# The turning frame of a state-space unit, from two tables of factors

## The chip, the cores and the metric

The kernel runs on one core of one Trainium2 chip. The metric is the device time of one execution in microseconds; the time of a kernel is the median of its runs, and the profiled execution's own time and span stand beside it. The engines are TensorE (PE, with its weight loads as PEld), VectorE (DVE), ScalarE (ACT), GpSimd (POOL) and SyncE (SP), which issues the DMAs.

## The reference, cut to what matters

One layer of a decoder for 512 tokens of width 2048 in float32: RMS norm, one input projection, two mixers side by side, an output projection with residual, a gated convolutional MLP, and a last norm. The change lies in the second mixer, S5, a diagonal state space of 64 groups with 64 complex states each:

```python
def s5_mixer(u, a_re, a_im, log_dt, b_re, b_im, c_re, c_im, d, w_glu, b_glu):
    A = lax.complex(a_re, a_im)
    dt = jnp.exp(log_dt)[:, None]
    A_bar = jnp.exp(A * dt)
    B_bar = ((A_bar - 1.0) / A)[..., None] * Bm
    Bu = jnp.einsum('gpc,btgc->btgp', B_bar, uf)
    ...
    _, states = lax.associative_scan(combine, (a, Bu), axis=1)
    y = jnp.real(jnp.einsum('gcp,btgp->btgc', Cm, states)) + d * uf
```

The recurrence `s[t] = A_bar s[t-1] + Bu[t]` is complex. The kernel runs it in a turning frame: `A_bar` is a size R times a turn `e^(i theta)`. Multiplied by the inverse of its own turn so far, the state follows a real recurrence with R alone, which DVE's scan instruction does for the real and the imaginary part; the result is turned back afterwards. Four tokens are taken together, so a step of the frame is the turn of four tokens, and there are 128 of them.

## The kernel before

**Matmuls.** Every float32 product is taken apart into a high and a low part and done as three matmuls (`mm3`, L208 to L210). ACT casts the high part of a weight chunk (L115), DVE subtracts for the low part (L116), and PE reads both. PE's work comes in dense chunks: first the projection `u` in two halves of four tiles (`upt`, 5 PSUM banks under the tag acc), then the other projections `xm`, `v`, `o`, later the output projection and the MLP.

**S5 beside it.** S5 is a Python generator, `s5()`, which the dense code advances by `pump()` after a chunk. So the engines' instruction orders are fixed when the program is built, and S5's small steps lie between dense chunks on each engine's queue. It begins with `s5_params()` (L360 to L441): from the parameters DVE works out the turn of one token for all 32 pairs of groups, and POOL squares it twice and then doubles it six times. That is the **EM chain** (L323 and L329 of POOL): seven levels of the turn by 1, 2, 4, ... 64 steps, real and imaginary, 32 columns each. They are kept in `prms`, one buffer of 512 columns, together with two weights `W0`.

**A unit.** Eight units of four pairs each follow. `phases(u)` (L463 to L489) makes the frame of a unit: `Er` and `Ei`, 4 pairs x 128 steps = 512 columns each, by doubling: one memset each, a copy of one step (L476, L477), then six levels of six POOL operations each (L482 to L487) which take the first m steps times the turn by m steps and write the next m. `Rd`, the sizes, is made by ACT (L468) and one memset of POOL (L469). The unit then makes its input coefficients (L515 to L528), multiplies them on PE into PSUM tiles `px` (L612), turns `px` by the frame on DVE (L619 to L624, into `vr`, `vi`), computes taps on PE (`pkt`, L636), scans and turns back (L639 to L648). `phases(u+1)` is called in the middle of unit u, just ahead of the buffers `ta`, `tb`, `vr`, `vi`; so the frame of a unit is made one unit ahead.

**Tokens.** When a half of `u` is complete, `u_tokens` evicts its four PSUM tiles, scaled, into four buffers `utok` (L293 to L300): even tiles by DVE (L300), odd ones by ACT (L298), four instructions each. The first half is evicted behind chunk 15, while PE goes on with the second half.

**Buffers.** `slot()` takes the oldest free buffer of 128x512 from a queue and `drop()` puts one back at its end. There are 13 float32 ones inside two larger areas, used first, and 60 more. A buffer that comes back from the queue makes its first writer wait for its last readers, whatever engine they are on.

## Time and profile before

| | us |
|---|---|
| median of 3 runs | 2100.53 (2099.14 to 2102.38) |
| profiled execution | 2100.77 |
| its span | 2099.0 |
| PE busy | 2055.1 |
| DVE busy | 1502.0 |
| ACT busy | 819.4 |
| POOL busy | 275.6, in 512 instructions |

The granted clock of PE is 0.99 over the whole span. PE is busy for 98% of it; the other engines are not, and what they do matters where PE waits for them. POOL's work lies mostly before 350 us, in the EM chain and the eight `phases`. The chain of waits that ended last is 83% PE and 9% DVE.

### The profile page before, as it was taken

What the parts mean: (1) busy time and instruction counts of PE and PEld (TensorE: products, weight loads), DVE (VectorE), ACT (ScalarE), POOL (GpSimd) and SP (SyncE); (2) the same over time, 40 slices, a digit from 0 to 9 for tenths busy, and PEclk for the clock granted to TensorE, in tenths of its full rate; (3) what the DMA queues carried; (4) which work ended last, traced back from release to release, by engine and by line L of the source; (5) the groups of instructions that cost most, each with busy time, mean ns of one, the idle gap of its engine ahead of it and who ended that gap; (6) DMA issues with size and microseconds to landing.
All of it is one profiled execution on the core that took longest, in us unless ns stands there. A gap on an engine that the chain in (4) does not pass through costs nothing.

```text
span 2099.0 us, 31618 instructions
## 1 busy us (share of the span) xinstructions
PE 2055.1 (98%) x12956; PEld 1874.6 (89%) x12956; DVE 1502.0 (72%) x2101; ACT 819.4 (39%) x1033; POOL 275.6 (13%) x512
## 2 busy tenths in 40 slices
PE   8999988999999999999999999999999999999997
PEld 8898877888888899999999999999999888888887
DVE  8698986557755799898899899889886544222235
ACT  5244332445423544444443444344343432211225
POOL 4874732002100200000000000000000000000003
PEclk9999999999999999999999999999999999999998
DMA  4222121222333423333333333433332555332352
GB/s 175 82 86 74 63 84 51 91 89 83 126 121 121 150 105 126 128 111 121 111 115 125 123 111 111 134 118 111 121 111 102 190 178 188 115 112 107 113 200 81
DMA packets 75370, 244.74 MB, mean 117 GB/s; under 512 B 8396, under 2 KB 14028, under 8 KB 64216
## 3 DMA queue, kind: packets, MB, share of 16 engines
q1 hardware_dynamic: 75224, 242.72, 33.8%
q8 instruction: 101, 1.65, 0.3%
q14 instruction: 45, 0.37, 0.1%
HBM read 220.12 MB, written 22.57 MB: 116 GB/s over the span
## 4 chain that ended last, share of the span: by engine, by line
PE 83%; DVE 9%; issue 3%; ACT 2%; POOL 2%; DMA 1%; SPq 0%; DVEq 0%; ACTq 0%; POOLq 0%
PE gv L210 14%; PE gv L208 14%; PE gv L209 14%; PE down L209 6%; PE down L210 6%; PE down L208 6%; DVE a L116 2%; PE o L208 1%; PE ws L208 1%; PE o L210 1%; PE ws L210 1%; PE o L209 1%; PE ws L209 1%; PE u L208 1%; PE u L209 1%
## 5 line engine op out<-in xcount | busy, mean ns | idle before, releaser
L210 PE MATMUL gv<-T,a 128*128 128x256 f32 x2408 | 682.2, 283 | 4.9 <-DVE a L1176 4.9
L208 PE MATMUL gv<-T,a 128*128 128x256 f32 x2408 | 682.1, 283 | 0.0
L209 PE MATMUL gv<-T,a 128*128 128x256 f32 x2408 | 682.0, 283 | 0.0
L1172 ACT CAST a<-a 128x1536 fp32r<-128x1536 f32 (+2 forms) x171 | 291.0, 1703 | 458.1 <-PE gv L209 295.7
L210 PEld LDWEIGHTS gv<-T,a 128*128 128x128 f32 x2408 | 463.0, 192 | 5.1 <-DVE a L1176 5.1
L208 PEld LDWEIGHTS gv<-T,a 128*128 128x128 f32 x2408 | 462.9, 192 | 0.0
L209 PEld LDWEIGHTS gv<-T,a 128*128 128x128 f32 x2408 | 462.9, 192 | 0.0
L116 DVE TENSOR_TENSOR a<-a,a 128x1024 fp32r<-128x1024 f32 (+2 forms) x207 | 241.1, 1169 | 288.3 <-ACT a L115 287.6
L1176 DVE TENSOR_TENSOR a<-a,a 128x1536 fp32r<-128x1536 f32 (+2 forms) x173 | 348.0, 2012 | 37.9 <-ACT a L1172 37.9
L115 ACT CAST a<-a 128x1024 fp32r<-128x1024 f32 (+2 forms) x208 | 199.8, 967 | 361.4 <-PE down L209 284.5
L1525 POOL TENSOR_TENSOR c<-c,c 128x256 f32<-128x256 f32 x24 | 17.7, 739 | 1318.5 <-ACT c L1523 1318.2
L208 PE MATMUL down<-c,a 128*128 128x512 f32 x448 | 174.5, 390 | 0.6 <-ACT c L115 0.6
L210 PE MATMUL down<-c,a 128*128 128x512 f32 x448 | 174.3, 389 | 0.0
L209 PE MATMUL down<-c,a 128*128 128x512 f32 x416 | 162.1, 390 | 0.9 <-DVE c L116 0.9
L1158 DVE TENSOR_TENSOR a<-a 128x1024 f32<-128x1024 f32 x85 | 103.6, 1219 | 0.0
L208 PEld LDWEIGHTS down<-c,a 128*128 128x128 f32 x448 | 84.1, 188 | 18.7 <-ACT c L115 1.4
L210 PEld LDWEIGHTS down<-c,a 128*128 128x128 f32 x448 | 84.1, 188 | 17.3
L209 PEld LDWEIGHTS down<-c,a 128*128 128x128 f32 x416 | 78.1, 188 | 17.7 <-DVE c L116 1.5
L209 PE MATMUL down<-a,a 128*128 128x512 f32 x176 | 68.5, 389 | 0.0
L208 PE MATMUL down<-a,a 128*128 128x512 f32 x176 | 68.5, 389 | 0.0
L1237 DVE SCALAR_TENSOR_TENSOR p<-p,vec,p 128x511 f32<-128x511 f32 x86 | 62.6, 748 | 2.5 <-ACT p L1230 0.9
L1164 DVE TENSOR_TENSOR a<-a 128x512 f32<-128x512 f32 x86 | 60.5, 704 | 2.9
(578 smaller groups left out, 3590.0 us busy)
## 6 DMA issues: line engine op xcount, KB each, us to landing
a<-in_wgv SPq DMA_DIRECT2D x86, 1024.0 KB, 4.8
a<-in_wdB SPq DMA_DIRECT2D x55, 512.0 KB, 3.5
a<-in_wdA SPq DMA_DIRECT2D x40, 320.0 KB, 3.1
hidd<-p SPq DMA_DIRECT2D x40, 256.0 KB, 5.4
a<-in_wxm SPq DMA_DIRECT2D x16, 512.0 KB, 3.2
a<-in_wv SPq DMA_DIRECT2D x16, 512.0 KB, 3.3
a<-in_wo SPq DMA_DIRECT2D x16, 512.0 KB, 3.3
a<-in_wouts SPq DMA_DIRECT2D x16, 512.0 KB, 3.5
```

What stands on the lines that cost most here:

```text
L115: S.copy(out=h, in_=src)
L116: V.tensor_tensor(out=l, in0=src, in1=f(h), op=SUB)
L208: PE.matmul(pt, lhsT=wh, rhs=xh, start=first, stop=False)
L209: PE.matmul(pt, lhsT=wh, rhs=xl, start=False, stop=False)
L210: PE.matmul(pt, lhsT=wl, rhs=xh, start=False, stop=last)
L1158: eng.tensor_tensor(out=v[:, 4:6], in0=v[:, 3:4].to_broadcast([P, 2, T]), in1=v[:, 0:2], op=ADD)
L1164: V.tensor_tensor(out=v[:, 3], in0=v[:, 6], in1=v[:, 2], op=ADD)
L1172: S.copy(out=part(RH[s % 2], lo, hi - lo), in_=part(RS[s % 2], lo, hi - lo))
L1176: V.tensor_tensor(out=part(RL[s % 2], lo, hi - lo), in0=part(RS[s % 2], lo, hi - lo), in1=f(part(RH[s % 2], lo, hi - lo)), op=SUB)
L1237: V.scalar_tensor_tensor(out=y1[:, s:], in0=gs[:, 0:T - s], scalar=vcol("f_cw", 3 * (k0 + j) + 2 - s), in1=y1[:, s:], op0=MUL, op1=ADD)
L1525: G.tensor_tensor(out=x2, in0=x2, in1=sq[:, 0:HT], op=ADD)
```

## The change

**Tables.** A frame of 128 steps is the product of two short ones: step 16a + b is step 16a times step b, with a from 0 to 7 and b from 0 to 15. `factors()` makes both tables once for all 32 pairs, at the end of the EM chain: `FB` (b, 16 entries x 32 pairs, 512 columns in each of two buffers) and `FA` (a, 8 entries x 32 pairs, real and imaginary halves of one buffer). Both come from `turns()`, the doubling of before with 32 pairs in place of 4: 46 instructions of POOL, four of them memsets. It then drops its scratch `gt` and `prms`; `W0` moves into spare columns of `cst`. Three buffers are held to the end of S5.

**Units.** `phases(u)` is now six operations of 512 columns, each with one factor broadcast along a and one along b; the memset and ACT's operation for `Rd` stay.

**Place.** `phases(u+1)` is called at the end of unit u, behind the drop of its buffers.

```diff
--- before.py
+++ after.py
@@ -357,6 +357,35 @@
 
     W0, EM, R4 = [], [], []
 
+    def turns(er, ei, lev0, n, gt):
+
+        G.memset(er[:, :, 0:1], 1.0)
+        G.memset(ei[:, :, 0:1], 0.0)
+        m, lev = 1, lev0
+        while m < n:
+            br, bi = [EM[lev][q].unsqueeze(2).to_broadcast([P, NPAIR, m]) for q in range(2)]
+            h1, h2 = [gt[:, o:o + NPAIR * m].rearrange("p (r n) -> p r n", r=NPAIR) for o in (0, 256)]
+            lo, hi = slice(0, m), slice(m, 2 * m)
+            G.tensor_tensor(out=h1, in0=er[:, :, lo], in1=br, op=MUL)
+            G.tensor_tensor(out=h2, in0=ei[:, :, lo], in1=bi, op=MUL)
+            G.tensor_tensor(out=er[:, :, hi], in0=h1, in1=h2, op=SUB)
+            G.tensor_tensor(out=h1, in0=er[:, :, lo], in1=bi, op=MUL)
+            G.tensor_tensor(out=h2, in0=ei[:, :, lo], in1=br, op=MUL)
+            G.tensor_tensor(out=ei[:, :, hi], in0=h1, in1=h2, op=ADD)
+            m, lev = 2 * m, lev + 1
+
+    FB, FA, held = [], [], []
+
+    def factors():
+
+        fbr, fbi, fa, gt = [slot(name=n) for n in ("fbr", "fbi", "fa", "gt")]
+        held.extend([fbr, fbi, fa])
+        FB.extend(t.rearrange("p (r b) -> p r b", r=NPAIR) for t in (fbr, fbi))
+        FA.extend(t.rearrange("p (r a) -> p r a", r=NPAIR) for t in (fa[:, 0:256], fa[:, 256:512]))
+        turns(*FB, 0, 16, gt)
+        turns(*FA, 4, 8, gt)
+        drop(gt, prms)
+
     def s5_params():
 
         a_re, a_im, ldt = vcol("a_re", 0, 32), vcol("a_im", 0, 32), vcol("log_dt", 0, 32)
@@ -409,6 +438,7 @@
             EM.append((er_, ei_))
             if lev < 6:
                 er_, ei_ = cmul(er_, ei_, er_, ei_, eng=G)
+        factors()
         c1 = tsc(cs, 1.0, SUB)
         cm1 = tt(c1, tt(tt(cm, c1, SUB), m0, MUL), ADD)
         yield
@@ -418,8 +448,8 @@
         pr_ = tt(tt(e1, cs, MUL), cm1, ADD)
         q1, q2, q3, q4 = tt(pr_, a_re, MUL), tt(ab_i, a_im, MUL), tt(ab_i, a_re, MUL), tt(pr_, a_im, MUL)
         q1, q3 = tt(q1, q2, ADD), tt(q3, q4, SUB)
-        W0.append(tt(q1, rden, MUL, o=keep()))
-        W0.append(tt(q3, rden, MUL, o=keep()))
+        W0.append(tt(q1, rden, MUL, o=cst[:, 288:320]))
+        W0.append(tt(q3, rden, MUL, o=cst[:, 320:352]))
         yield
 
         a2r, a2i = cmul(ab_r, ab_i, ab_r, ab_i, af(0, 1), af(1, 1))
@@ -464,27 +494,15 @@
 
             pr = slice(4 * u, 4 * u + 4)
             er_, ei_, gt, Rd = [slot(name=n) for n in ("Er", "Ei", "gt", "Rd")]
-            er, ei = v3(er_), v3(ei_)
+            er, ei, h = [t.rearrange("p (r a b) -> p r a b", r=4, a=8) for t in (er_, ei_, gt)]
             S.activation(out=v3(Rd), in_=R4[0][:, pr].unsqueeze(2).to_broadcast([P, 4, P]), func=AF.Copy)
             G.memset(v3(Rd)[:, :, 0:1], 0.0)
-            G.memset(er[:, :, 0:1], 1.0)
-            G.memset(ei[:, :, 0:1], 0.0)
-            for lev in range(7):
-                m = 1 << lev
-                br, bi = EM[lev][0][:, pr].unsqueeze(2), EM[lev][1][:, pr].unsqueeze(2)
-                if lev == 0:
-                    G.tensor_copy(er[:, :, 1:2], br)
-                    G.tensor_copy(ei[:, :, 1:2], bi)
-                    continue
-                br, bi = br.to_broadcast([P, 4, m]), bi.to_broadcast([P, 4, m])
-                h1, h2 = v3(gt[:, 0:4 * m]), v3(gt[:, 256:256 + 4 * m])
-                lo, hi = slice(0, m), slice(m, 2 * m)
-                G.tensor_tensor(out=h1, in0=er[:, :, lo], in1=br, op=MUL)
-                G.tensor_tensor(out=h2, in0=ei[:, :, lo], in1=bi, op=MUL)
-                G.tensor_tensor(out=er[:, :, hi], in0=h1, in1=h2, op=SUB)
-                G.tensor_tensor(out=h1, in0=er[:, :, lo], in1=bi, op=MUL)
-                G.tensor_tensor(out=h2, in0=ei[:, :, lo], in1=br, op=MUL)
-                G.tensor_tensor(out=ei[:, :, hi], in0=h1, in1=h2, op=ADD)
+            ar, ai = [t[:, pr, :].unsqueeze(3).to_broadcast([P, 4, 8, 16]) for t in FA]
+            br, bi = [t[:, pr, :].unsqueeze(2).to_broadcast([P, 4, 8, 16]) for t in FB]
+            for o, (x1, y1), (z1, w1), op in ((er, (ar, br), (ai, bi), SUB), (ei, (ar, bi), (ai, br), ADD)):
+                G.tensor_tensor(out=o, in0=x1, in1=y1, op=MUL)
+                G.tensor_tensor(out=h, in0=z1, in1=w1, op=MUL)
+                G.tensor_tensor(out=o, in0=o, in1=h, op=op)
             drop(gt)
             return er_, ei_, Rd
 
@@ -613,8 +631,6 @@
                     px.append(p_)
                 drop(*XB)
                 Er, Ei, Rd = nxt
-                if u < 7:
-                    nxt = phases(u + 1)
                 ta, tb, vr, vi = slot(name="ta"), slot(name="tb"), slot(name="vr"), slot(name="vi")
                 V.tensor_tensor(out=ta, in0=px[0], in1=Er, op=MUL)
                 V.tensor_tensor(out=vi, in0=px[0], in1=Ei, op=MUL)
@@ -647,8 +663,10 @@
             V.tensor_tensor(out=rb, in0=e_i, in1=s_r, op=MUL)
             V.tensor_tensor(out=v3(Si)[:, :, 1:P], in0=ra, in1=rb, op=SUB)
             drop(ta, tb, vr, vi, Rd, Er, Ei)
+            if u < 7:
+                nxt = phases(u + 1)
             yield
-        drop(*const, afs, prms)
+        drop(*const, afs, *held)
 
 
     pg = []
```

Three places of the instruction order follow. The first is DVE, where chunk 15 of `u` ends and the first half is evicted (`u_0`, `u_2` are PSUM tiles, `r_c` the scale, `a_73` one of the larger areas that hold 13 buffers, `utok_...` a buffer of its own). Before:

```order
L116 TENSOR_TENSOR a_70<-a_68,a_69 128x1024 [waits DMAHW6_49,Activation_49]
L300 TENSOR_SCALAR a_73<-u_0_107,r_c 128x4x32 [waits DVE_49,PE_49]
L300 TENSOR_SCALAR utok_657<-u_0_107,r_c 128x4x32
L300 TENSOR_SCALAR utok_659<-u_0_107,r_c 128x4x32
L300 TENSOR_SCALAR utok_661<-u_0_107,r_c 128x4x32
```

After:

```order
L116 TENSOR_TENSOR a_70<-a_68,a_69 128x1024 [waits DMAHW6_49,Activation_49]
L300 TENSOR_SCALAR a_73<-u_0_107,r_c 128x4x32 [waits DVE_49,PE_49,Pool_49]
L300 TENSOR_SCALAR a_73<-u_0_107,r_c 128x4x32
L300 TENSOR_SCALAR utok_708<-u_0_107,r_c 128x4x32
L300 TENSOR_SCALAR utok_710<-u_0_107,r_c 128x4x32
```

The number of rows and their place is the same; the first L300 gains a wait on Pool, and the second utok has moved into the area `a_73` too. The same place on ACT (tiles `u_1` and `u_3`), before:

```order
L115 CAST a_69<-a_68 128x1024 [waits DMAHW6_49,PE_49]
L298 ACTIVATE a_73<-u_1_108,r_c 128x4x32 [waits DVE_49,PE_49,Pool_49]
L298 ACTIVATE utok_657<-u_1_108,r_c 128x4x32
L298 ACTIVATE utok_659<-u_1_108,r_c 128x4x32
L298 ACTIVATE utok_661<-u_1_108,r_c 128x4x32
```

After:

```order
L115 CAST a_69<-a_68 128x1024 [waits DMAHW6_49,PE_49]
L298 ACTIVATE a_73<-u_1_108,r_c 128x4x32 [waits DVE_49,PE_49,Pool_49]
L298 ACTIVATE a_73<-u_1_108,r_c 128x4x32
L298 ACTIVATE utok_708<-u_1_108,r_c 128x4x32
L298 ACTIVATE utok_710<-u_1_108,r_c 128x4x32
```

The first L298 has a wait on Pool in both; the second has moved into the area. On POOL the end of the EM chain and what follows it, before:

```order
L329 TENSOR_SCALAR scr_600<-scr_600 128x32 [waits Pool_49]
L323 TENSOR_TENSOR a_73<-scr_600 128x32 [waits Pool_49]
L323 TENSOR_TENSOR a_73<-scr_600 128x32
L469 MEMSET Rd_808 128x4 [waits DMAHW6_49,Activation_49]
L470 MEMSET Er_805 128x4 [waits DMAHW3_49]
L471 MEMSET Ei_806 128x4
L476 COPY Er_805<-a_73 128x4
L477 COPY Ei_806<-a_73 128x4
L482 TENSOR_TENSOR gt_807<-Er_805,a_73 128x8 [waits Pool_49]
```

After:

```order
L329 TENSOR_SCALAR scr_600<-scr_600 128x32 [waits Pool_49]
L323 TENSOR_TENSOR a_73<-scr_600 128x32 [waits Pool_49]
L323 TENSOR_TENSOR a_73<-scr_600 128x32
L362 MEMSET fbr_609 128x32
L363 MEMSET fbi_610 128x32
L369 TENSOR_TENSOR gt_612<-fbr_609,a_73 128x32 [waits Pool_49]
L370 TENSOR_TENSOR gt_612<-fbi_610,a_73 128x32 [waits Pool_49]
L371 TENSOR_TENSOR fbr_609<-gt_612 128x32 [waits Pool_49]
L372 TENSOR_TENSOR gt_612<-fbr_609,a_73 128x32 [waits Pool_49]
```

The tables of L362 to L374 stand where unit 0's frame stood; 38 more rows of them follow, then unit 0's (L499 to L505). On DVE, the first products of unit 6, before:

```order
L116 TENSOR_TENSOR a_70<-a_68,a_69 128x1024 [waits DMAHW3_49,Activation_49]
L619 TENSOR_TENSOR ta_2974<-px,Er_2576 128x512 [waits DMAHW0_49,PE_49]
L620 TENSOR_TENSOR vi_2977<-px,Ei_2577 128x512 [waits Pool_49]
L621 TENSOR_TENSOR tb_2975<-px,Ei_2577 128x512 [waits PE_49]
L622 TENSOR_TENSOR vr_2976<-ta_2974,tb_2975 128x512 [waits DVE_49]
L623 TENSOR_TENSOR tb_2975<-px,Er_2576 128x512 [waits DVE_49]
```

After (the lines are the former L619 to L622):

```order
L116 TENSOR_TENSOR a_70<-a_68,a_69 128x1024 [waits DMAHW3_49,Activation_49]
L635 TENSOR_TENSOR ta_2730<-px,a_73 128x512 [waits PE_49]
L636 TENSOR_TENSOR vi_2733<-px,p_76 128x512
L637 TENSOR_TENSOR tb_2731<-px,p_76 128x512 [waits PE_49]
L638 TENSOR_TENSOR vr_2732<-ta_2730,tb_2731 128x512 [waits DMAHW0_49,DVE_49]
L639 TENSOR_TENSOR tb_2731<-px,a_73 128x512 [waits DVE_49]
```

The wait of `vi` on Pool is no longer there.

## Rows read from the trace of the kernel before

**Rows 1.** The page, part 1: busy us (share of span) x instructions, each engine.

```profile
PE 2055.1 (98%) x12956; PEld 1874.6 (89%) x12956; DVE 1502.0 (72%) x2101; ACT 819.4 (39%) x1033; POOL 275.6 (13%) x512
```

**Rows 2.** Windows: length, each engine's busy us (x instructions), granted PE clock, DMA share, GB/s.

```profile
61.10:67.20 6.10, 6.10 (x16) 4.91 (x17) 4.31 (x17) 0.52 (x2) 5.77 (x23) 0.51 0.20 64
67.40:73.50 6.10, 6.10 (x27) 6.10 (x27) 2.79 (x7) 2.58 (x7) 5.76 (x23) 1.00 0.15 54
331.00:337.00 6.00, 5.91 (x28) 4.56 (x29) 5.64 (x13) 0.15 (x1) 0.00 (x0) 0.52 0.00 0
350.00:2099.00 1749.00, 1729.65 (x11326) 1590.66 (x11324) 1211.94 (x1527) 680.65 (x785) 72.81 (x62) 1.00 0.36 122
```

**Rows 3.** PE's waits, 30 to 400 us: in total, times, longest.

```profile
PE v L209 <- DVE a L116: 7.9, 3, 4.6
PE pkt L636 <- DVE vi L620: 5.8, 1, 5.8
```

**Rows 4.** Timeline of PE in S5's part (start us, us, instruction, [idle before]).

```profile
268.75 0.79 PE L209 MATMUL v<-a,xh 128*128 128x512 f32 x1 [2.16 <-DVE a L116]
...
300.52 0.79 PE L209 MATMUL v<-a,xh 128*128 128x512 f32 x1 [4.59 <-DVE a L116]
...
347.38 0.50 PE L209 MATMUL v<-a,xh 128*128 128x512 f32 x1 [1.12 <-DVE a L116]
```

**Rows 5.** Timeline of PE, the second half of u.

```profile
70.93 0.39 PE L208 MATMUL u<-a,a 128*128 128x512 f32 x1
```

**Rows 6.** Timeline of DVE: the utok writes, the next split, unit 0's first product.

```profile
64.86 0.34 DVE L300 TENSOR_SCALAR a<-u,r_c 128x128 f32<-128x128 f32 x1
...
71.83 1.36 DVE L116 TENSOR_TENSOR a<-a,a 128x1024 fp32r<-128x1024 f32 x1 [2.39 <-ACT a L115]
...
99.92 0.69 DVE L619 TENSOR_TENSOR ta<-px,Er 128x512 f32<-128x512 f32 x1 [8.96 <-POOL Er L484]
```

**Rows 7.** Timeline of ACT: its utok writes of the first half.

```profile
66.69 0.37 ACT L298 ACTIVATE a<-u,r_c 128x128 f32<-128x128 f32 x1 [9.00 <-POOL scr L323]
67.01 0.89 ACT L298 ACTIVATE utok<-u,r_c 128x128 f32<-128x128 f32 x3
```

**Rows 8.** Timeline of POOL: three of the starts of an EM level.

```profile
67.59 0.46 POOL L323 TENSOR_TENSOR a<-scr,scr 128x32 f32<-128x32 f32 x2
...
70.41 0.47 POOL L323 TENSOR_TENSOR a<-scr 128x32 f32<-128x32 f32 x2
...
84.99 0.76 POOL L323 TENSOR_TENSOR a<-scr 128x32 f32<-128x32 f32 x2
```

**Rows 9.** Timeline of POOL: phases(0), level starts, and the start of phases(1).

```profile
85.69 0.10 POOL L469 MEMSET Rd<- 128x4 f32 x1
...
91.41 0.24 POOL L482 TENSOR_TENSOR gt<-Er,a 128x32 f32<-128x32 f32 x1
...
93.11 0.29 POOL L482 TENSOR_TENSOR gt<-Er,a 128x64 f32<-128x64 f32 x1
...
95.15 0.40 POOL L482 TENSOR_TENSOR gt<-Er,a 128x128 f32<-128x128 f32 x1
...
96.52 0.40 POOL L485 TENSOR_TENSOR gt<-Er,a 128x128 f32<-128x128 f32 x1
...
97.89 0.61 POOL L482 TENSOR_TENSOR gt<-Er,a 128x256 f32<-128x256 f32 x1
...
101.91 0.11 POOL L469 MEMSET Rd<- 128x4 f32 x1
```

**Rows 10.** POOL's groups by line and shape, 40 to 110 us.

```profile
L976 POOL TENSOR_TENSOR a<-a,sq 128x512 f32<-128x512 f32 x5 | 6.6, 1311 | 10.7 <-ACT sq L975 6.0 <-ACT wg L115 4.7
```

**Rows 11.** Timeline of DVE in units 5 and 6.

```profile
286.98 1.77 DVE L116 TENSOR_TENSOR a<-a,a 128x1024 fp32r<-128x1024 f32 x1
...
330.25 0.69 DVE L620 TENSOR_TENSOR vi<-px,Ei 128x512 f32<-128x512 f32 x1 [11.03 <-POOL Ei L487]
...
346.12 1.21 DVE L116 TENSOR_TENSOR a<-a,a 128x1024 fp32r<-128x1024 f32 x1
```

## The prediction

> **What bounds the kernel now.** I read the page's table of engines first, then PE's waits, then PE beside the other engines around each wait. PE is busy for 2055.1 of 2099.0 us [rows 1]; DVE, ACT and POOL all have room, so a change on POOL counts only where PE comes to wait for it. From 350 us to the end PE is busy for 1729.65 of 1749 us at full clock [rows 2], and I found no wait there that S5 causes. Two kinds of wait between 50 and 400 us matter [rows 3]: PE pkt for DVE's vi, once, 5.8 us, and PE v for DVE's L116, three times, 7.9 us, at 268.75, 300.52 and 347.38 [rows 4]. After a long idle PE runs at the lower of its two clock levels (granted 0.51, about 1.2 GHz): 16 matmuls in 6.1 us at 61.1, where it does 27 at 67.4 with 1.00 [rows 2]. That is (27-16)/27 x 6.1 = 2.5 us lost; 331 to 337 reads the same (0.52). I price the clock behind a long stall at 2.6.
>
> **The change, its early end.** Per unit, 38 operations and 3 memsets become six operations and one memset. That is what the edit names; what PE sees first is something else. `factors()` puts 46 instructions on POOL right behind the EM chain and then drops `prms`, the buffer of the EM tables, before `u_tokens` asks for its first buffer. The pool of buffers is first in, first out and empty of older ones there, so utok 0 is now that very buffer. The order rows show it: DVE's first L300 gains a wait on Pool, and ACT's first L298, which had one on an older and finished POOL operation, now writes the same buffer. Column by column, DVE's write covers the real part of EM's last level, read last by the fifth operation of the tables' last doubling (L373); ACT's covers the imaginary part, read last by the fourth (L372). So DVE stops at 64.86 and ACT at 66.69 [rows 6, 7] until POOL is nearly through, with everything queued behind them: the evictions of `u`, the splits L115/L116, the `dg` scaling, the S5 parameters. PE's second half of `u` is the victim: there are five banks, it can start the fifth, and its matmul at 70.93 [rows 5] needs ACT's four L298 out first, the next tile DVE's four L300.
>
> When is POOL through? One EM level takes 70.41-67.59 = 2.82 us while DVE is quiet; the four from 70.41 to 84.99 took 3.65 each beside DVE's work [rows 8]. DVE stands still in after, so 70.41 + 4 x 2.82 + 0.47 = 82.2. The tables are levels of six operations, and unit 0's phases have the same widths on a quiet POOL [rows 9]: 32 columns 93.11-91.41 = 1.70, 64 columns 2.04, 128 columns 2.74, 256 columns 4.02. The table of 16 takes all four, 10.50; that of eight takes 1.70 + 2.04 and then, to the end of its last level's fourth operation, 96.92-95.15 = 1.77; memsets 0.2. ACT is let go at 82.2 + 10.5 + 0.2 + 3.74 + 1.77 = 98.4, DVE 0.4 later. ACT's four L298 last 1.21 (66.69 to 67.90) [rows 7], so PE resumes at about 99.7 in place of 70.93: **+28.7**, and **+2.6** for the clock. I see no second stall behind it: DVE restarts slightly ahead of PE, and of its old idle time the 2.39 ahead of L116 [rows 6] shows that it was not the late one.
>
> Bounds for this term: if EM keeps its old pace it ends at 85.7 [rows 9] (+3.5). The tables' operations run over 32 short runs of columns where the timed ones had four. A contiguous 128x32 operation of EM (two in 0.46 [rows 8]) costs what 32 columns in four runs cost (0.24 [rows 9]), so runs were free up to there; for 32 of them no row stands, and I allow 0 to 5, taking 0. Below, POOL would have to beat its quiet rows, so 27 at least.
>
> **What unit 0 gives back: nothing.** DVE waited 8.96 us for Er at 99.92 [rows 6]. In after the six operations stand ready, as phases(0) is 6 x 1.31 = 7.9 us by the row of a 128x512 operation [rows 10] in place of 101.91-85.69 = 16.2 [rows 9], and waits only for ACT's Rd. But PE was not idle there: its waits list one for pkt in all, unit 6's [rows 3]. The wait disappears beside work that hides it.
>
> **What the later units give back.** In before, vi's buffer in unit 6 is the gt that phases(7) had just dropped: DVE did ta, then waited 11.03 us until POOL was through with phases(7) [rows 11], and PE's pkt waited 5.8. The order rows show vi without that wait in after, because phases(u+1) is now called at the unit's end. Gone: 5.8 and the clock behind it (2.5), **-8.3**. The third L116 wait (1.12 at 347.38 [rows 4]) is DVE running late behind that stall: **-1.2**; Rd moves with the call, on ACT past L568, an L115 and L638 to behind the scans, ahead of the next L115, which could give up to 1 back. On POOL the units' phases have nothing else of weight between them to pass. The 4.59 at 300.52 [rows 4]: DVE is late there at the end of unit 5, partly because phases(6) ran beside it (L116 1.77 at 286.98 against 1.21 at 346.12 [rows 11]; some five such operations, 2 to 3 us). phases(6) now runs after the scans, beside a few short operations and one L116, which costs about 1.3 again: **-1.5**, between 0 and -3, or -7 with the clock if it vanished. The first L116 wait (2.16 at 268.75) I leave as it is, since phases(5) still runs beside the split ahead of it: 0, from -2 to +1.5. At nothing: W0 in another buffer (same two writes), three buffers held through S5 (the pool is deep enough that no new late wait shows), and SP, whose order is unchanged and whose fetches run ahead of their use; without that lead a fetch would cost what the last user of its buffer is late.
>
> **Sum.** 28.7 + 2.6 - 8.3 - 1.2 - 1.5 = +20.3 on the profiled execution's 2100.77 (span 2099.0 and 1.8 around it; 0.24 above the median of 2100.53): **2121**. Its own range is 2115 to 2126.
>
> **A page against the rows.** Beside POOL, DVE's L116 grew by 0.56 [rows 11], and beside DVE an EM level of twelve POOL operations grew by 0.83 [rows 8]: both are slowed in part. The Trainium skill (SBUF — State Buffer, "Who interferes with whom") says instead that the port pair DVE shares with GpSimd is an exclusive lock held for the whole instruction, so that the loser fully blocks. By it the longer operations would hold DVE back longer, not shorter, and the sum would be that of the third rival, worked out there from rows.
>
> **Rivals.**
> 1. POOL slower than the quiet rows: EM at its old pace and short rows dear, +8: **2129**. For it: 32 rows are in no trace. Against: one to four runs cost the same.
> 2. The late gains fail: the splits on ACT wait for Rd behind the scans and PE stalls again near 330 to 347, so 8.3 and 1.2 stay: **2130.5**. Against: Rd's wait ends with scans that ACT's next split nearly waits for anyway.
> 3. A POOL operation of 512 columns blocks DVE for its whole length: five of phases(6) fall beside the end of DVE's chain at 300, up to 1.3 each, 6.5, less the 2.5 that go: +4 in place of -1.5, **2126.5**. Against: the partial slowing above.
> 4. The other side, **2090**: the wait on Pool is for an earlier operation than I derive, one that is over before PE gets to 70.93; then only the gains stay, 2100.8 - 11.0. For it: the order names the engine waited for, not its instruction. The point that decides is POOL releasing the buffer before about 78, when stall and clock just eat the 11 us. Against: the buffer is that of the tables which the last L373 reads, and EM alone ends past 82.
>
> **How the numbers follow.** Forecast 0.68, rival 1 0.11, rival 2 0.08, rival 3 0.05, rival 4 0.06, anything else 0.02. The likeliest time is 2121. The range leaves out rival 4 and the ends: low 2113 (the tables 2 shorter, the stall at 300 and its clock all but gone, -6), high 2131 (rivals 1 and 2). A measurement of this kernel can tell about 0.2%, 4 us, from no change: faster by more has 0.06, all of it rival 4; within, 0.03, a mix of an early release and full gains; slower 0.91.
>
> **What would show it.** In the trace of after: a DVE wait of about 34 us ahead of the first L300, released by POOL gt L373; ACT's at L298 by L372; PE idle about 28.7 us after the sixth matmul of the fifth tile, then 0.5 clock for 6 us; tables of 16 to 18 us; six POOL operations of about 1.3 us per unit; no PE wait for pkt, and DVE's wait of 11 us gone. I am wrong if DVE's first L300 starts near 65, if POOL's table levels are far from the 1.70 to 4.02 of the rows, or if PE still waits some 6 us for a pkt near 355 (331 moved by the shift).

## The result, and the profile after

The changed kernel takes 2130.07 us, median of 3 runs (2129.06 to 2130.63), against 2100.53: a ratio of 1.0142 [1.0128, 1.0156], slower by 29.5 us where the forecast said 20.3. Its profiled execution took 2130.63 us with a span of 2128.9, so the spans differ by 29.9; that is what is taken apart here. Page, part 1, of after, which answers to [rows 1]:

```profile
PE 2055.8 (97%) x12956; PEld 1875.2 (88%) x12956; DVE 1516.4 (71%) x2101; ACT 819.1 (38%) x1033; POOL 206.2 (10%) x286
```

PE has the same work. POOL has 69 us less of it. DVE has not one instruction more or less (x2101 in both) and is busy 14.4 us longer; the prediction has no term for that.

The early stall stands where it was put. Timeline of after, POOL, ACT, DVE and PE around it: the first operation of the tables, the last three that matter, and who they let go (start us, us, instruction, [idle before <- what ended it]):

```profile
83.17 0.26 POOL L369 TENSOR_TENSOR gt<-fbr,a 128x32 f32<-128x32 f32 x1
...
99.36 0.41 POOL L372 TENSOR_TENSOR gt<-fa,a 128x128 f32<-128x128 f32 x1
99.73 0.41 POOL L373 TENSOR_TENSOR gt<-fa,a 128x128 f32<-128x128 f32 x1
99.81 0.62 ACT L298 ACTIVATE a<-u,r_c 128x128 f32<-128x128 f32 x2 [41.19 <-POOL gt L372]
100.18 0.61 DVE L300 TENSOR_SCALAR a<-u,r_c 128x128 f32<-128x128 f32 x2 [34.30 <-POOL gt L373]
...
101.00 0.82 PE L208 MATMUL u<-a,a 128*128 128x512 f32 x1 [29.17 <-ACT utok L298]
```

DVE's utok write, at 64.86 before [rows 6], starts at 100.18, released by L373; ACT's is released by L372; PE stands for 29.17 us where [rows 5] has the next matmul without a wait. PE's other waits from 110 us on that are over 1 us, from the same timeline; the last two are the counterparts of the first two of [rows 4], while the pkt wait and the third of [rows 4] are gone:

```profile
121.71 0.63 PE L618 MATMUL pw<-ident,p 128*128 128x128 f32 x4 [1.21 <-DVE p L537]
...
256.64 0.50 PE L210 MATMUL xm<-xh,a 128*128 128x512 f32 x1 [2.23 <-DVE a L116]
...
305.91 0.50 PE L209 MATMUL v<-a,xh 128*128 128x512 f32 x1 [3.94 <-DVE a L116]
...
339.07 0.79 PE L209 MATMUL v<-a,xh 128*128 128x512 f32 x1 [5.81 <-DVE a L116]
```

Where the 29.9 us came from is best seen by one event that occurs once in every unit. This table has the start of the pkt matmuls in each kernel's timeline of PE, and how far after lies behind before:

| unit | 0 | 3 | 4 | 5 | 6 | 7 | end of span |
|---|---|---|---|---|---|---|---|
| before, us | 104.19 | 208.61 | 243.97 | 283.33 | 331.09 | 370.35 | 2099.0 |
| after, us | 137.16 | 241.58 | 279.46 | 320.66 | 363.52 | 398.79 | 2128.9 |
| behind, us | 33.0 | 33.0 | 35.5 | 37.3 | 32.4 | 28.4 | 29.9 |

So 33.0 us are lost by unit 0, nothing in units 1 to 3, 4.4 more in units 4 and 5, and only then 8.9 come back. In the 1730 us behind unit 7 another 1.5 us appear, without any wait on PE that differs; I take them for scatter between executions (before's runs lie 3.2 us apart), which is not shown.

### The profile page after: what moved, and what is told of

The parts are those of the page before. It is cut to its first block, busy times and chain, and to the rows that moved or that the text cites. A ratio compares the mean times of both kernels' runs of the same rounds, so it can differ in the third digit from the quotient of the medians.

```text
span 2128.9 us, 31385 instructions
## 1 busy us (share of the span) xinstructions
PE 2055.8 (97%) x12956; PEld 1875.2 (88%) x12956; DVE 1516.4 (71%) x2101; ACT 819.1 (38%) x1033; POOL 206.2 (10%) x286
## 4 chain that ended last, share of the span: by engine, by line
PE 81%; DVE 10%; ACT 2%; issue 1%; DMA 0%; SPq 0%; DVEq 0%; ACTq 0%
PE gv L210 14%; PE gv L208 14%; PE gv L209 14%; PE down L209 6%; PE down L210 6%; PE down L208 6%; DVE a L116 2%; PE o L208 1%; PE ws L208 1%; PE o L210 1%; PE ws L209 1%; PE o L209 1%; PE ws L210 1%; PE v L209 1%; PE v L208 1%
## 5 line engine op out<-in xcount | busy, mean ns | idle before, releaser
L116 DVE TENSOR_TENSOR a<-a,a 128x1024 fp32r<-128x1024 f32 (+2 forms) x206 | 242.4, 1181 | 286.5 <-ACT a L115 285.7
L1543 POOL TENSOR_TENSOR c<-c,c 128x256 f32<-128x256 f32 x24 | 17.7, 738 | 1319.3 <-ACT c L1541 1318.4
```

Source lines behind the costliest of these rows:

```text
L116: V.tensor_tensor(out=l, in0=src, in1=f(h), op=SUB)
L1543: G.tensor_tensor(out=x2, in0=x2, in1=sq[:, 0:HT], op=ADD)
```

## How DVE came to be busy longer

Here is one DVE operation with POOL beside it in after, first DVE's timeline, then POOL's. L116 is the split that PE waits for at 256.64:

```profile
253.16 1.43 DVE L664 TENSOR_TENSOR Si<-vr,vi 128x508 f32<-128x508 f32 x1
254.52 2.07 DVE L116 TENSOR_TENSOR a<-a,a 128x1024 fp32r<-128x1024 f32 x1
...
254.01 1.49 POOL L504 TENSOR_TENSOR gt<-fa,fbi 128x512 f32<-128x512 f32 x1
255.58 2.15 POOL L505 TENSOR_TENSOR p<-p,gt 128x512 f32<-128x512 f32 x1
```

Add starts and durations. POOL's L504 ends at 255.50. L116 lasts 1.21 alone [rows 11] and ends here at 254.52 + 2.07 = 256.59, that is 1.09 behind L504's end: it did next to nothing until POOL was through. POOL's L505 starts at 255.58 and ends at 257.73, 1.14 behind L116's end: now POOL waited. They take turns, by whole operations. The smallest DVE operations show it too. Same timelines, at the end of unit 5, where the operations on 16 columns take 0.17 us each when POOL is idle (the last two rows are the same operations in before, with no POOL operation beside them):

```profile
330.40 1.03 DVE L329 TENSOR_SCALAR lsig<-lsig 128x16 f32<-128x16 f32 x1
331.47 0.25 DVE L730 RECIPROCAL lsig<-lsig 128x16 f32<-128x16 f32 x1
331.76 2.05 DVE L323 TENSOR_TENSOR lsig<-lsig 128x16 f32<-128x16 f32 x2
333.85 0.98 DVE L329 TENSOR_SCALAR lsig<-lsig 128x16 f32<-128x16 f32 x1
334.86 2.79 DVE L334 SCALAR_TENSOR_TENSOR lsig<-lsig 128x16 f32<-128x16 f32 x9
...
329.90 1.50 POOL L504 TENSOR_TENSOR gt<-fa,fbi 128x512 f32<-128x512 f32 x1
331.48 1.29 POOL L505 TENSOR_TENSOR a<-a,gt 128x512 f32<-128x512 f32 x1
332.72 1.06 POOL L503 TENSOR_TENSOR p<-fa,fbi 128x512 f32<-128x512 f32 x1
333.74 1.05 POOL L504 TENSOR_TENSOR gt<-fa,fbr 128x512 f32<-128x512 f32 x1
...
296.14 0.17 DVE L329 TENSOR_SCALAR lsig<-lsig 128x16 f32<-128x16 f32 x1
297.25 1.84 DVE L334 SCALAR_TENSOR_TENSOR lsig<-lsig 128x16 f32<-128x16 f32 x9
```

POOL's operations end at 331.40, 332.77, 333.78 and 334.79; DVE's at 331.43, 333.81 (its first half near 332.8) and 334.83. Each of these DVE operations lasts as long as what was left of one POOL operation and ends 0.03 or 0.04 us behind it. The L730 between starts 0.01 ahead of a POOL operation and lasts its usual 0.25.

And before did the same. The L116 of 1.77 us in [rows 11], from which the prediction read a slowing in part, stood beside this one (timeline of POOL, before):

```profile
286.90 0.76 POOL L484 TENSOR_TENSOR Er<-gt 128x256 f32<-128x256 f32 x1
```

It ends at 287.66, and 287.66 + 1.09 = 288.75 = 286.98 + 1.77. The 0.56 that the prediction took for a slowing in part fits a full wait for the rest of a short operation. Longer POOL operations make that rest longer.

## The experiments

The theories. **A**: the early stall is the reuse of the EM tables' buffer, and nothing else costs much. **B**: the late waits are an echo of the early stall (DVE and ACT come out of it late). **C**: POOL's longer operations hold DVE for their whole length, and the late waits come from there. **D**: not the arithmetic but the place of the call decides what is won late. All ratios are against the kernel before on the same chip.

### The early stall: e1_keep_buffer, e2_unit0_doubled

Both start from after. The first keeps the EM tables to the end, so that no later tile gets their buffer:

```
-        drop(gt, prms)
+        drop(gt)
...
-        drop(*const, afs, *held)
+        drop(*const, afs, prms, *held)
```

> The changed kernel with one thing undone: the buffer of the EM tables is kept to the end of S5, so that utok 0 gets another buffer. My theory: the wait of DVE's and ACT's first utok writes on POOL (34.3 and 41.2 us) and PE's 29.2 us with the slow clock behind it, 31.8 in all, are gone, but the tables still stand ahead of unit 0's frame on POOL: the EM chain ends near 86 beside a working DVE, the tables near 104, unit 0's vi is ready some 10 later, and PE's pkt, which came at 104.2 in the kernel before, waits 11 to 14 us, with 2.5 of slow clock behind it: about 2113 (2108 to 2117). Rival: unit 0's frame is covered by other work once the buffer is not reused, and the whole 31.8 goes: 2098. If the buffer is not the cause: still about 2130.

Measured: 2106.57 us, 1.0031 [1.0021, 1.0040], 1.4 us below the range that was expected. The wait for utok is gone and with it 23.5 of the 29.5 us. What remains early is unit 0's frame, which now queues on POOL behind the tables (timeline of DVE, then PE, of this run):

```profile
107.28 0.69 DVE L635 TENSOR_TENSOR p<-px,Er 128x512 f32<-128x512 f32 x1 [18.65 <-POOL Er L505]
...
111.49 0.30 PE L591 MATMUL pk<-ident,a 128*128 128x128 f32 x1 [3.12 <-DVE vi L636]
113.53 1.09 PE L479 MATMUL pu<-ident,utok 128*128 128x128 f32 x4 [1.75 <-DVE a L639]
```

I had expected the pkt of unit 0 to wait for vi. It did not: pk and pu waited, as I read it for the PSUM banks that DVE frees. A is right on the buffer, but not on the rest: the tables that stand ahead of unit 0 on POOL cost too. The second run takes that away too: unit 0 doubles its frame with the 38 operations of before (their code comes back and is left out here), and the tables are built behind it.

```
-        factors()
...
         nxt = phases(0)
+        factors()
```

> As e1, and in addition unit 0's frame is made by the doubling of the kernel before, straight behind the EM chain, with the tables behind it; units 1 to 7 use the tables as in the changed kernel. So nothing early stands in the way, and the stretch from 240 to 350 us is seen alone. Theory of the port lock (each POOL operation of 512 columns holds DVE back for its whole 1.3 us, and phases(u+1) at the unit's end lies just ahead of DVE's splits that PE waits for): the three late waits of the changed kernel, 2.2, 3.9 and 5.8 us with their clock, stay, the pkt wait of 5.8 and the 1.1 stay away: about 2098 (2095 to 2102). Rival, that the late waits of the changed kernel are an echo of the 30 us shift: they go back to the 2.2 and 4.6 of before or less, about 2090.

Measured: 2101.83 us, 1.0008 [0.9998, 1.0017]. Another 4.7 us go. Of the early waits that before does not have, one of 1.5 us is left (u for an L116 of DVE, at 116.45), and PE still has these late ones (PE's waits between 30 and 450 us: total, times, longest):

```profile
PE v L209 <- DVE a L116: 9.7, 2, 5.8
PE xm L210 <- DVE a L116: 3.0, 1, 3.0
```

They are after's waits (9.7 in two and 2.2 in one), so B falls: they stand without the early stall. DVE is busy for 1513.8 us here, 11.8 over before. The six products per unit, with the early cost removed, win nothing.

### Place or arithmetic: e3_before_late, e4_scan_target_last, e5_tables_mid

The first is the kernel before with the call alone moved to where after has it; the doubling stays:

```
                 Er, Ei, Rd = nxt
-                if u < 7:
-                    nxt = phases(u + 1)
...
             drop(ta, tb, vr, vi, Rd, Er, Ei)
+            if u < 7:
+                nxt = phases(u + 1)
```

> The kernel before, with only the place of phases(u+1) moved to the end of unit u; frames are made by doubling, 38 operations. Both theories: the pkt wait of 5.8, its clock and the 1.1 go, -9.5. Theory of the place (POOL work of any operation length at the unit's end holds DVE's short operations): the late waits on L116 grow as in the changed kernel or more, since the doubling keeps POOL busy for longer: 2096 to 2100. Theory of the long operations (only 512 columns at a time do harm): they stay at 2.2 and 4.6 or shrink: about 2090.

Measured: **2089.82 us, 0.9944 [0.9928, 0.9960]**: faster than both kernels, and the best version of the study that computes everything. DVE is busy for 1492.7 us, 9.3 less than before. PE's waits between 30 and 450 us, those of S5:

```profile
PE v L209 <- DVE a L116: 5.5, 3, 4.8
...
PE pk L573 <- ACT a L636: 1.9, 1, 1.9
...
PE pkt L634 <- DVE vi L618: 0.8, 1, 0.8
```

The 5.8 for pkt [rows 3] and the first wait of [rows 4] are gone, the second stands at 4.77 and the third at 0.46; the 0.8 is new, ahead of unit 4's pkt at 242.95, and the wait of pk behind it grew from 0.4 to 1.9. So the gain that the prediction gave to the change belongs to the place of the call. The late place also suits the doubling: its first levels are of 0.2 us each, and they are what runs beside DVE's chain at the unit's end. Timeline of DVE and POOL at that place (compare 334.86 in after, where nine L334 took 2.79):

```profile
294.02 1.90 DVE L334 SCALAR_TENSOR_TENSOR lsig<-lsig 128x16 f32<-128x16 f32 x9
296.07 1.23 DVE L116 TENSOR_TENSOR a<-a,a 128x1024 fp32r<-128x1024 f32 x1
...
295.35 0.24 POOL L485 TENSOR_TENSOR gt<-p,a 128x16 f32<-128x16 f32 x1
...
296.18 1.22 POOL L482 TENSOR_TENSOR gt<-p,a 128x32 f32<-128x32 f32 x1
```

Here POOL is the one held: its operation on 32 columns, 0.24 in [rows 9], takes 1.22, until L116 is through.

The second removes the pkt wait in another way: the call stays, but vr, tb and vi are taken ahead of it, so that the buffer that the call drops goes to ta, the target of the scan.

> The kernel before, with the place and the doubling kept; only the buffers of the unit are taken in another order: vr, tb, vi ahead of phases(u+1), ta (now only the scan's target) behind it, and the first product is written into vr. So the buffer gt that phases has just dropped is waited for at the scan and not at the second product. Expected: the 5.8 us wait of pkt and its clock go, DVE's wait moves to the scan and is about 3 us instead of 11, the 1.1 stays or goes: 2091 to 2093. The waits of 2.2 and 4.6 stay. If the pkt wait has another cause than this buffer: 2100.

Measured: 2102.08 us, 1.0008 [0.9999, 1.0018], a miss. The wait only moved down DVE's chain (timeline of DVE, then PE):

```profile
335.94 1.22 DVE L640 TENSOR_TENSOR_SCAN ta<-Rd,vr 128x512 f32<-128x512 f32 x1 [8.51 <-POOL Ei L487]
...
343.74 0.80 PE L209 MATMUL v<-a,xh 128*128 128x512 f32 x1 [7.25 <-DVE a L116]
```

The third is e2 with the call in the middle of the unit (for units 0 to 5; the last one stays late for want of buffers), ta taken behind it.

> The kernel of the second experiment (unit 0 by doubling, tables behind it, units 1 to 7 from the tables) with phases(u+1) back in the middle of the unit for units 0 to 5 (for unit 6 the buffers don't suffice, there it stays at the end), and the scan's target as the last buffer taken. Theory of the lock: DVE's products of px, which come next there, read PSUM and one SBUF operand and are not held back, and POOL is through in 8 to 10 us, before the scans; so the late waits fall to those of the kernel before at most (2.2 and 4.6) and the 3.0 goes: 2088 to 2093. If operations of 512 columns do the same harm wherever they stand beside DVE: still about 2100.

Measured: 2097.65 us, 0.9994 [0.9984, 1.0003], DVE busy 1507.7: a miss, 5 us above the top of what was expected. Side by side, with the early cost in none of them, each as its ratio to the kernel before on its own chip and DVE's busy us:

| | call in mid-unit | call at the unit's end |
|---|---|---|
| doubling, 38 operations | 1 (before), 1502.0 | 0.9944 (e3), 1492.7 |
| products, 6 operations | 0.9994 (e5), 1507.7 | 1.0008 (e2), 1513.8 |

D holds only with C: the late place is worth 0.56% with short operations, some 11 us, and gains nothing with long ones (0.14% the other way, which the intervals don't separate; e5 differs from e2 by its order of buffers too, so that is not the place alone).

### What holds DVE: e6_no_frames, e10_memsets, e10b_products

The first gives the price of seven of the eight frames: units 1 to 7 use unit 0's.

> The kernel before without the frames of units 1 to 7: they reuse unit 0's Er and Ei, so this leaves out the 38 POOL operations of seven units, and only Rd is made for each. It shows what all of POOL's frames cost, and what of the late waits belongs to DVE alone. Theory of the lock: the pkt wait (5.8), the 1.1 and most of the 2.2 at 269 go with POOL's work; of the 4.6 at 300 some 2 to 3 us go: 2081 to 2086. If POOL's operations cost DVE little: only the 9.5 us of the buffer wait go: 2091.

Measured: 2079.74 us, 0.9902 [0.9887, 0.9917], 1.3 us below the range that was expected; DVE busy 1483.2, and of the late waits one of 0.72 us is left. So seven frames, on an engine that is busy for 13% [rows 1], cost the kernel before some 19 us, the wait of pkt for a buffer included. The next two put POOL work back into this kernel, at the unit's end, with results that nothing reads: fifteen memsets in one, six products in the other.

```
+                gt = slot(name="gt")
+                for _ in range(15):
+                    G.memset(gt, 0.0)
```

> As the sixth experiment (units 1 to 7 reuse unit 0's frame, which leaves out their 38 POOL operations), with 15 memsets of 128x512 by POOL at the end of each of seven units, 7.7 us of POOL's time per unit, about what six products take. If POOL holds the shared ports only with operations that read SBUF: DVE's busy time and the total stay as without frames, 1483 and 2080 (2077 to 2082). If any POOL operation holds them: as with the products of its twin, 2085 to 2095.

Measured: 2078.49 us, 0.9902 [0.9888, 0.9916], as expected for POOL operations that hold only when they read; DVE busy 1483.7. Timeline of DVE and POOL, the last row an operation of DVE beside another unit's memsets:

```profile
248.66 0.69 DVE L656 TENSOR_TENSOR vr<-Er,tb 128x508 f32<-128x508 f32 x1
250.58 1.22 DVE L116 TENSOR_TENSOR a<-a,a 128x1024 fp32r<-128x1024 f32 x1
...
248.05 8.71 POOL L474 MEMSET gt<- 128x512 f32 x15
...
287.08 0.44 DVE L329 TENSOR_SCALAR lsig<-lsig 128x16 f32<-128x16 f32 x1
```

8.7 us of POOL in this unit, and DVE's operations with two inputs have their lengths of a quiet POOL. There is an exception, and it is small: L329, with one tile in and one out, takes 0.44 here and 0.42 at 288.26, where it takes 0.17 without memsets, and both end 0.03 us behind the end of a memset (287.49 and 288.65). So a memset did hold this kind of operation.

```
+                gt = slot(name="gt")
+                for _ in range(6):
+                    G.tensor_tensor(out=gt, in0=frame0[0], in1=frame0[1], op=MUL)
```

> The twin of the memsets: units 1 to 7 reuse unit 0's frame (their own is left out), and POOL does six products of 512 columns of that frame into a spare buffer at the end of each of seven units, which nothing reads. Theory of the lock: DVE's busy time rises by 3 to 4 us per unit, from 1483 to 1505 to 1512, and the late waits of 3.0, 3.9 and 5.8 us come back in good part, as the products wait for nothing: 2088 to 2096. If the waits came from the frames being late and not from the ports: 2080.

Measured: 2115.09 us, 1.0073 [1.0058, 1.0087]; DVE busy 1523.0. Timeline of DVE, POOL and PE:

```profile
227.03 1.66 DVE L656 TENSOR_TENSOR vr<-Er,tb 128x508 f32<-128x508 f32 x1
231.95 2.28 DVE L116 TENSOR_TENSOR a<-a,a 128x1024 fp32r<-128x1024 f32 x1
234.15 0.68 DVE L774 TENSOR_TENSOR xs<-xm,r_bc 128x512 f32<-128x512 f32 x1
...
224.97 10.38 POOL L474 TENSOR_TENSOR gt<-Er,Ei 128x512 f32<-128x512 f32 x6
...
234.28 0.80 PE L210 MATMUL xm<-xh,a 128*128 128x512 f32 x1 [5.60 <-DVE a L116]
```

L656 takes 1.66 where it took 0.69, L116 2.28 where it took 1.22. PE's waits for L116 under v and xm come to 16.0 us in four and 7.6 in three, where the run with memsets has one of 1.2. No wait of DVE or PE is released by these products (one of ACT is, 5.1 us in the first unit, and the memsets release the same one after 4.9), and they cost 36.6 us over the memsets, more than I had expected. This shows C: what costs is POOL's products, which read the tiles' memory (SBUF), and not POOL being busy; no semaphore between DVE and POOL is involved. That they cost more than e2's own six per unit has a likely reason, which was not tested apart: they begin earlier, beside four operations of 508 columns (L655 to L658, most of them 1.6 to 1.8 us long), while the frame in after first waits for a buffer that the second of those four still reads (POOL idle for 8.02 us ahead of L503 at 252.62). L774, one of whose inputs comes straight from PE's matmul, runs in its usual 0.68 beside the same POOL operations.

### Can it be cured: e7_after_taps, e8_halves, e9_eighths, e11_late_pieces

The first three start from e2. e7 calls `phases` behind the next unit's taps instead of at the unit's end:

```
                 taps()
+                if u < 8:
+                    nxt = phases(u)
```

> The kernel of the second experiment with phases(u+1) called one step later, behind the taps of the next unit: POOL's six operations then no longer stand ahead of the last splits (L116) and the taps of unit u, but beside the coefficients of unit u+1. Theory of the place: the waits of 3.0, 3.9 and 5.8 us shrink by what POOL held DVE there (to about 0.5, 1 and 4.6), and DVE's coefficients are late by up to 7 us where they follow, which PE's pw may wait for by 1 to 3 us in some units: 2090 to 2097. If the place does not matter: 2101.

Measured: 2096.7 us, 0.9987 [0.9977, 0.9996], DVE busy 1508.0, in the expected range. PE's late waits change their place (3.5 and 3.6 us are the longest) and do not go: the products now hold DVE's three operations on y, 4.69 us (at 155.44) where they last 2.32. e8 makes each operation two of 256 columns, e9 eight of 64:

> The kernel of the second experiment with each of the six operations split into two of 256 columns, the place unchanged. If a POOL operation holds a DVE operation back for its whole length, one for one, then twice as many DVE operations are held for half as long: for the many short ones at 300 to 310 the sum stays (5.8 stays within 1), for the few long ones around 226 and 275 it falls (3.0 and 3.9 to about 2): 2096 to 2100. If only the length of an operation counted: half of the 12 us that lie between the second and the third experiment, 2096 or less. If length plays no part at all: 2101 to 2102.

Measured: 2098.5 us, 0.9998 [0.9989, 1.0008], DVE busy 1512.0: in the expected range, 0.1% below e2, which the intervals don't separate, and still no gain.

> The kernel of the second experiment with each of the six operations split into eight of 64 columns, 48 in all, at the same place. Theory of the lock (a DVE operation that needs the shared ports waits for one POOL operation to its end, then they take turns): a DVE operation is now held for about 0.3 us at a time; DVE's busy time, 1513.8 with 512 columns and 1512.0 with 256, falls to 1500 or less, and the late waits to those of the third experiment: 2091 to 2096. POOL's own time for a frame rises from 8 to some 14 us, which nothing waits for. If it is POOL's total time beside DVE that counts: 2098 or more.

Measured: 2105.41 us, 1.0027 [1.0016, 1.0037], a miss. DVE's busy time fell to 1493.3, as the theory has it, and POOL's rose to 312.6. Timeline of POOL, PE and ACT:

```profile
226.90 4.29 POOL L526 TENSOR_TENSOR p<-fa,fbr 128x64 f32<-128x64 f32 x8 [9.05 <-DVE vr L688]
...
145.60 0.43 PE L678 MATMUL pkt<-a 128*32 128x128 f32 x8 [4.03 <-DVE vi L662]
...
289.45 3.79 PE L656 MATMUL px<-U,xb 128*128 128x128 f32 x16 [5.22 <-ACT xb L646]
...
288.81 1.07 ACT L646 COPY xb<-pw 128x512 f32<-128x512 f32 x2 [10.29 <-POOL a L530]
```

Eight operations of 64 columns take 0.54 each beside DVE, twice their 0.27 alone; now POOL loses the turns, and the frame is late: at 145.60 PE's pkt waits for vi, which waits for POOL. The larger part of PE's waits is px for ACT's copy xb, 11.9 us in five. That copy reads no frame, yet it is let go by POOL's last operation on one; I take it to wait for a buffer that POOL still read, which is not shown. e11 tried the same on the best version, e3, with each level cut into pieces of at most 64 columns:

> The third experiment (doubling, phases(u+1) at the unit's end, 2089.8) with the three last levels cut into operations of at most 64 columns (4 pairs x 16 steps). Theory of the lock: DVE is held for 0.3 us at a time in place of up to 0.8; DVE's busy time falls from 1492.7 to 1487 to 1490, and the time to 2085 to 2089. If the small operations only make the frame late, units would wait for it: above 2090.

Measured: 2107.8 us, 1.0039 [1.0026, 1.0052], a miss. DVE's busy time is 1486.7, as expected; but POOL, at 311.4, is late (timeline of POOL, DVE, PE; the second row is what DVE did meanwhile):

```profile
277.99 3.40 POOL L488 TENSOR_TENSOR p<-gt 128x64 f32<-128x64 f32 x1
...
278.19 2.34 DVE L116 TENSOR_TENSOR a<-a,a 128x1024 fp32r<-128x1024 f32 x2
...
290.78 0.69 DVE L618 TENSOR_TENSOR ta<-px,p 128x512 f32<-128x512 f32 x1 [4.38 <-POOL p L488]
...
294.72 0.43 PE L635 MATMUL pkt<-a 128*32 128x128 f32 x8 [2.00 <-DVE vi L619]
```

One operation of 64 columns, 0.41 a few rows later, took 3.40: DVE ran two L116, an L516 and an L517 in that time, one right behind the other, the last to 281.21, and POOL's ended at 281.39. Cutting moves the hold from DVE to POOL, and DVE waits at the next frame instead. I found no size of piece that wins on both sides; e3's mixture of short and long levels is the best that ran.

## Why the prediction was right, and where it was not

- **The stall ahead of u: right.** 28.7 forecast, 29.17 measured (29.3 from start to start of PE's matmuls), by the mechanism and the instructions named (L372 for ACT, L373 for DVE). EM ended at 82.9 against 82.2, the tables took 17.7 us (82.94 to 100.67), and their 32 short rows cost next to nothing extra (the level of 32 columns 1.79 in place of 1.70, that of 256 4.03 in place of 4.02): the bound of 0 to 5 was rightly taken at 0. e1 shows the buffer as the cause.
- **The clock behind it: too dear.** 2.6 forecast, 1.9 measured. Nine matmuls ran at the lower level, from 101.00 to 105.03, 4.03 us in which before does nine from 70.93 on in 2.12; the next ones are 0.24 apart. The windows say the same: 18 matmuls from 100.9 to 107.0 at a granted 0.66, where [rows 2] has 16 at 0.51 and 27 at 1.00, so (27-18)/27 x 6.1 = 2.0. The 33.0 us of unit 0 are then 0.8 by which after was late ahead of the change already (71.44 against 70.69 for the last matmul ahead of the stall), 29.3, 1.9 and 1.0 for pw.
- **Unit 0 gives back nothing: it costs 1.0.** PE's pw at 121.71 waits 1.21 for an L537 of DVE that ran beside phases(0), two in 2.35 us where two take 0.85 elsewhere.
- **The gains of units 6 and 7: right.** -8.3 and -1.2 forecast. After falls from 37.3 to 28.4 us behind in these units, and that contains 1.2 the other way at 339.07: 10.1 against 9.5. But e3 shows that they belong to the call's place, not to the products.
- **Contention: the step that failed.** -1.5 forecast; measured +2.5 up to unit 4's pkt (a new wait of 2.23 at 256.64), +1.8 up to unit 5's (3.94 against 2.16) and +1.2 up to unit 6's (5.81 against 4.59), +5.5 in all. The prediction argued that phases(6) would run beside a few short operations and one L116, "which costs about 1.3 again". Those short operations lost 4.3 us: L329, two L323, L329 and nine L334 took 1.03, 2.05, 0.98 and 2.79 us, where the same groups of before, from 296.14 on with no POOL operation beside them, took 0.17, 0.38, 0.17 and 1.84. It also left the wait at 268.75 as it was, within +1.5, and saw none ahead of xm, though POOL's frame comes to the end of those units too. e10b shows that such products alone, without any buffer or late frame, make these waits.
- **The rule that the prediction set aside.** The Trainium skill (SBUF — State Buffer, "Who interferes with whom") says that a DVE instruction with two SBUF inputs contends with a GpSimd instruction that reads SBUF and not with one that only writes, and that the loser blocks for the whole of the other's instruction. The runs agree on each point: 0.69 against 1.66 us with products beside it, 0.69 with memsets, and ends that lie 0.03 to 0.04 us (short operations) or 1.09 (L116) behind POOL's. They show one more thing, that L329, with one input, is held by products and by memsets. I weighed that rule against durations alone and read 0.56 as a slowing in part; had I added up start and duration of the two rows, the DVE operation's end would have stood 1.09 behind POOL's. The other row that it read so fits too: in before one POOL operation of an EM level took 1.22 us, where its neighbours take 0.25, beside the L116 at 71.83 [rows 6], and ended 0.10 behind it. Rival 3 had the mechanism, at 0.05, but priced it at one place in one unit.
- **The sum.** 9.6 us lie between the forecast of +20.3 and the +29.9 of the spans: contention 7.0, pw 1.0, the late start 0.8, the stall 0.6, less 0.7 for the clock and 0.6 for the gains, and 1.5 behind S5 that no wait explains. Rivals 1, 2 and 4 did not occur. That the time is close to rival 1 and rival 2 is chance: POOL was not slower, and the late gains came. And that it still lies below the 2131 of the range is luck: that end was set for these two rivals, and contention, which the prediction had the wrong way round, took their place. The early end is right nearly throughout; of the -11.0 of the late end there came -4.6 (28.4 us behind in place of 33.0).

What stays open: what the late 4.8 us for v in e3 would need to go (without the frames, in e6, they are 0.7), whether products could win at a place where DVE reads only PE's results, and whether a POOL operation that reads one tile holds DVE as a product of two does; none was tried.

## What to carry to other kernels

Before work is moved on POOL, list DVE's operations that will run beside it and charge each one that has no input from PE's results with the rest of one POOL operation. Here fewer and longer operations cut POOL's busy time by a quarter and still cost; the sign was DVE's busy time, which grew with no instruction added. When a buffer is dropped earlier in program order, look for the next tile that gets it and at what its last reader is queued behind. And try a move of the call and a change of the arithmetic apart: here the first alone gave 0.9944, and the second took all of that away (e2, 1.0008).

## What the hardware showed that I had not expected

- A DVE operation whose inputs are tiles in SBUF and a product of POOL wait for each other's whole operations, with no semaphore between them: operations of 0.17 us on DVE take 0.98 to 1.03 beside POOL's operations of 512 columns, and a POOL operation of 0.24 takes 1.22 beside L116. It is no strict alternation: several DVE operations in a row can pass one of POOL (3.40 in e11).
- Operations of POOL that only write hold next to nothing: fifteen memsets of 128x512 per unit left DVE's busy time at 1483.7 (1483.2 without them), and six products of the same size made it 1523.0. What memsets did hold is L329, a TENSOR_SCALAR: 0.44 and 0.42 us in place of 0.17.
- A DVE operation with an input straight from a PE result was not held: 0.68 us for xs<-xm,r_bc in the middle of e10b's products.
- How soon PE's granted clock was back at 1.00 does not follow the idle ahead of it. In after it took 4.1 us from the first matmul behind an idle of 29.17 (101.00), in before 5.6 us behind the 5.78 ahead of pkt (331.09). The stretch at 61.1 of [rows 2], lower for another 5.9 us, comes behind an idle of 2.58 and sixteen matmuls of 2 columns, so not behind a long idle, as the prediction has it. No run here shows what makes the difference.
